# A chunked RWKV-7 scan: block-diagonal exponentials, operand products over 128 partitions, and inverse blocks placed by DMA

## The chip, the cores and the metric

The kernel runs on one core of a Trainium2 chip. A core has five engines with instruction streams of their own: TensorE (PE in the profile, with its weight loads as PEld), VectorE (DVE), ScalarE (ACT), GpSimd (POOL) and SyncE (SP), which in this kernel mostly starts DMAs. The metric is the device time of one execution in microseconds (us), the median over runs. All five engines wait for each other through semaphores.

## The reference, cut to what matters

One layer of a diffusion backbone: layer norms with modulation, one input projection that feeds three token mixers (Mamba-2 SSD, RWKV-7, GLA), an output projection, then a mixture of 64 experts. The change lies in the RWKV-7 mixer, a linear recurrence with a state of 64x64 per head, four heads, run forward and backward over 2304 tokens:

```python
def step(S, inp):
    r_t, w_t, k_t, v_t, kk_t, a_t = inp
    sa = -jnp.einsum('nhvk,nhk->nhv', S, kk_t)
    S = S * w_t[:, :, None, :] + sa[..., None] * (kk_t * a_t)[:, :, None, :] + v_t[..., None] * k_t[:, :, None, :]
    return S, jnp.einsum('nhvk,nhk->nhv', S, r_t)
y = unboth(_rwkv7_scan(both(r, r), both(w_f, w_b), both(k_f, k_b), both(v, v), both(kk, kk), both(a_f, a_b)))
```

Everything is computed in float32.

## The kernel before, in words

The kernel doesn't step through tokens. It cuts the 2304 tokens into 18 segments of 128 tokens, each of four chunks of 32. A segment of the forward direction (d=0) and one of the backward direction (d=1) are handled together as a pair, so there are 18 pairs in `run` (L609).

For each pair there is a preparation and a chain. The **chain** (`chain`, L624, and `chunk`, L646) carries the state through the four chunks of both directions: small matmuls, each waiting for a copy on ACT or an update on DVE of the one before, in 24 hops per pair. The **preparation** (`prep`, L494) makes, for the next pair, what the chain needs and the state doesn't enter:

- `first` (L522): cumulative sums of the log decays (L533, DVE; L534, POOL), their exponentials `rkE` (L536) and `rkEi` (L540) on ACT, and the operands `rkar` and `rkbk`, products of the loaded inputs `rkX` with these exponentials. The operands are stored block-diagonally by head: for heads in partitions 0-63 one set of columns, for those in 64-127 another, with zeros elsewhere that are written once. So a product covers 64 partitions. Per direction there are 8 of them on DVE (L548, L549) and 8 on POOL (L551, L550).
- `grams` (L554): PE products of the operands (L563), masked on DVE (L567, L569, L570), summed on POOL (L572) and stored to DRAM (L573). `btrans` (L575) transposes `rkbk` on PE.
- An inverse of 16x16 triangular blocks, for both directions at once: load of the blocks (L504), start value copied from a constant identity (L508), 30 small DVE operations in strict sequence (L513, L514), a transposed copy (L515), two stores to the DRAM buffer `rkTd` (L517).
- `diag` (L585), per direction: a load of the inverse blocks (`rkDT`, L588, 128x8x16), and a POOL multiplication by a 0/1 mask `hk` that spreads them block-diagonally over 128x1024 elements (`rkD`, L591).
- `inv1` (L595) and `inv2` (L602): two groups of matmuls per direction with `rkD` (L598, L605) that assemble the inverse of the 32x32 blocks, an ACT copy between them (`rkW`, L600) and a DVE subtraction behind them (`rkTb`, L607).

`PLAN` (L623) says at which hop of the chain the preparation takes a step. PE's order in this stage is fixed by hand: hops, preparation steps, and between them matmuls of the input projection for the other two mixers (L184, L203; `FILL`, 4, 3 or 4 matmuls per hop), which keep PE busy during the waits of the chain. So an instruction on PE that waits holds up all of these behind it. The orders of DVE, ACT, POOL and SP are made by a scheduler at build time from the program and its priorities. SP starts nearly all DMAs of the stage: inputs `rkX` (L489), values `rkuv` (L529), outputs `rkY` (L645), and the stores of the projection (`fo`, L189). The chain begins at its first hop with the operands of the pair; the D matmuls (L598) stand at hops 22 and 23 of the pair before.

Of the kernel before, what the change touches and what calls it, by code (L numbers as in the profile page):

```python
# [25 lines left out]
def ap(t, off, dims):  # L26
    return bass.AP(tensor=t.tensor, offset=t.offset + off, ap=[list(d) for d in dims])
# [377 lines left out]
def rk_masks(nc, pool, tmp):  # L405

    M={}
# [9 lines left out]
    hk=pool.tile([128,4,2],F32,name='hk')
    for q in range(4):
        for k in range(2):
            nc.vector.tensor_scalar(hk[:,q,k:k+1],h,float(q),None,op0=OP.is_equal)  # L420
            t=tmp.tile([128,1],F32,name=f'rkhk{q}{k}'); nc.vector.tensor_scalar(t,bs,float(k),None,op0=OP.is_equal)
            nc.vector.tensor_tensor(hk[:,q,k:k+1],hk[:,q,k:k+1],t,op=OP.mult)
    M['hk']=hk

    blk=tmp.tile([128,32],F32,name='blk16'); nc.vector.tensor_scalar(blk,bt[:,:32],bs,None,op0=OP.is_equal)
    for d in range(1):
        st=tmp.tile([128,128],F32,name=f'rkst{d}'); nc.vector.tensor_scalar(st,I,s,None,op0=(OP.is_gt if d==0 else OP.is_lt))
        ge=tmp.tile([128,128],F32,name=f'rkge{d}'); nc.vector.tensor_scalar(ge,I,s,None,op0=(OP.is_ge if d==0 else OP.is_le))

        lo=pool.tile([128,32],F32,name=f'mlo{d}'); nc.vector.tensor_tensor(lo,st[:,:32],blk,op=OP.mult)  # L430
        M['lo',d]=lo

        of=tmp.tile([128,32],F32,name=f'rkof{d}'); nc.vector.tensor_tensor(of,st[:,:32],lo,op=OP.subtract)
        m=pool.tile([128,2,32],F32,name=f'moff{d}')
        mi=tmp.tile([128,2,32],F32,name=f'mincl{d}')
        ms=tmp.tile([128,2,32],F32,name=f'mstr{d}')
        for half in range(2):
            P=slice(64*half,64*half+64)
            b=bd[P,64*half:64*half+64].rearrange("p (h t)->p h t",h=2)
            nc.vector.tensor_tensor(m[P],b,of[P,None,:].to_broadcast([64,2,32]),op=OP.mult)  # L440
            nc.vector.tensor_tensor(mi[P],b,ge[P,:64].rearrange("p (h t)->p h t",h=2),op=OP.mult)
            nc.vector.tensor_tensor(ms[P],b,st[P,:64].rearrange("p (h t)->p h t",h=2),op=OP.mult)
        M['off',d]=m

        gk=pool.tile([128,2,2,2,32],F32,name=f'mgk{d}')
        nc.vector.memset(gk,0.0)
        for p in range(2):
            B=slice(64*p,64*p+64); K=slice(64-64*p,128-64*p)
            nc.vector.tensor_copy(gk[K,p,p],ms[K])
            nc.vector.tensor_copy(gk[K,p,1-p],mi[K])  # L450
            nc.vector.tensor_copy(gk[B,p,1-p],mi[B])
        M['gk',d]=gk
        rm=pool.tile([128,8,32],F32,name=f'rm{d}')
        nc.vector.memset(rm,1.0)
        e=0 if d==0 else 31
        nc.vector.memset(rm[:,:,e:e+1],0.0)
        M['rm',d]=rm
# [3 lines left out]
class Rwkv:  # L461


    def __init__(s, tc, nc, const, sb, ps, dram, M, ident, OPS, V, Y, T):
        s.tc=tc; s.nc=nc; s.sb=sb; s.ps=ps; s.M=M; s.id=ident; s.OPS=OPS; s.V=V; s.Y=Y; s.T=T; s.dram=dram
        s.S=[None,None]
        s.st={}

        s.bufs={}; s.cnt={}
        for n,w,k in (('ar',1024,4),('bk',1024,2),('lf',512,2),('uv',512,4)):  # L470
            s.bufs[n]=[]; s.cnt[n]=0
            for i in range(k):
                t=const.tile([128,w],F32,name=f'rk{n}{i}')
                nc.gpsimd.memset(t,0.0)
                s.bufs[n].append(t)
        for d in range(2):
            s.S[d]=[const.tile([128,3,64],F32,name=f'rkS{d}{i}') for i in range(2)]
            for t in s.S[d]: nc.vector.memset(t,0.0)
        s.eye=const.tile([64,256],F32,name='rkI'); nc.gpsimd.memset(s.eye,0.0); nc.gpsimd.memset(s.eye[:,0:256:17],1.0)
    def buf(s,n):  # L480
        l=s.bufs[n]; t=l[s.cnt[n]%len(l)]; s.cnt[n]+=1
        return t
# [11 lines left out]
    def prep(s,segs):  # L494

        nc=s.nc; sb=s.sb
# [8 lines left out]
        Tn=sb.tile([64,2,16,16],F32,name='rkTn',bufs=1)  # L505
        tmp=sb.tile([64,64],F32,name='rktm',bufs=1)
        X0=Tn[:,0]
        nc.vector.tensor_copy(X0.rearrange("p a b->p (a b)"),s.eye)  # L508
        for j in range(15,0,-1):

            nr=j; ncl=16-j
# [10 lines left out]
    def first(s,d,seg):  # L522
# [7 lines left out]
        A=sb.tile([128,2,2,4,32],F32,name='rkA',bufs=1)  # L530
        cs=A[:,0].rearrange("p a u t->p a (u t)"); csx=A[:,1].rearrange("p a u t->p a (u t)")
        for p in range(2):
            nc.vector.tensor_tensor_scan(cs[:,p],M['rm',0].rearrange("p a t->p (a t)")[:,0:128],Xr[:,4,p],0.0,op0=OP.mult,op1=OP.add)  # L533
        nc.gpsimd.tensor_tensor(csx,cs,Xr[:,4],op=OP.subtract)  # L534
        E=sb.tile([128,2,2,4,32],F32,name='rkE',bufs=1)
        nc.scalar.activation(E.rearrange("p e a u t->p (e a u t)"),A.rearrange("p e a u t->p (e a u t)"),AF.Exp)  # L536
        G=sb.tile([128,2,4],F32,name=f'rkG{d}')
        nc.vector.tensor_copy(G,E[:,0,:,:,31])
        Ei=sb.tile([128,2,4,32],F32,name='rkEi',bufs=1)
        nc.scalar.activation(Ei.rearrange("p a u t->p (a u t)"),cs.rearrange("p a t->p (a t)"),AF.Exp,scale=-1.0)  # L540

# [12 lines left out]
    def grams(s,d,Ld,R):  # L554
# [29 lines left out]
        R.append(BKt)  # L584
    def diag(s,d,Td):  # L585
        nc=s.nc; sb=s.sb; M=s.M
        DT=sb.tile([128,2,4,16],F32,name='rkDT')
        nc.sync.dma_start(DT.rearrange("p a u j->p (a u) j"),ap(Td,d*16384,[[16,128],[2048,8],[1,16]]))  # L588
        D=sb.tile([128,8,4,2,16],F32,name='rkD',bufs=2)
        DTv=DT.rearrange("p a u j->p (a u) j")  # L590
        nc.gpsimd.tensor_tensor(D.rearrange("p au h k j->p au (h k) j"),DTv[:,:,None,:].to_broadcast([128,8,8,16]),  # L591
            M['hk'].rearrange("p h k->p (h k)")[:,None,:,None].to_broadcast([128,8,8,16]),op=OP.mult)
        Dv=D.rearrange("p (a u) h k j->p a u (h k j)",a=2)
        return Dv
    def inv1(s,d,R,Dv):  # L595
        nc=s.nc; lfm=R[4].rearrange("p (u c)->p u c",u=4)
# [82 lines left out]
class Ssd:  # L679
# [117 lines left out]
    def evac(s, pool, i, o, P, g):  # L797
# [1076 lines left out]
```

## Time and profile before

| what | value |
|---|---|
| three runs | 3887.36, 3897.21, 3893.46 us; median 3893.46 us |
| the profiled execution's own time | 3880.03 us |
| its span on the core | 3878.3 us |
| mean granted PE clock over the span | 0.947 of full |
| PE / DVE / ACT / POOL busy, share of the span | 90% / 68% / 43% / 33% |
| the scan stage | from about 647 to 1402 us of the span |
| its 17 preparations that run beside a chain | the first ends at about 695 us, the last at about 1388 us |

The times of the profile are microseconds from the start of the span. Busy time is summed over an engine's instructions; the idle time of an engine before an instruction is put down to what released it. PE's matmuls are pipelined, so a busy PE may be busy at less than its peak. The scan is one of several stages. The first 647 us project the input and prepare the RWKV inputs, the stage behind the scan (1402 to about 2055 us) does the SSD and GLA mixers and the output projection, and the rest is the mixture of experts. None of the others touches the changed lines, though the convolution of the projection shares the `fh` buffer (L806).

### The profile page before, as it was taken

The numbers are of one execution on the slowest core, as the hardware profiler recorded it, in microseconds if no ns is written. First come the engines' busy times: TensorE is split into PE (matmuls) and PEld (weight loads), VectorE is DVE, ScalarE is ACT, GpSimd is POOL, SyncE is SP. The second block draws the span as 40 slices with busy tenths as digits, with TensorE's granted clock in tenths as the row PEclk, the third lists the DMA queues.
The fourth block names the chain that finished last, engine by engine and source line by source line (L and its number), as shares of the span: only waits on it lengthen the run. The fifth ranks groups of instructions, "written<-read, shape, count | busy, mean of one in ns | idle before, by whom it ended". The sixth has DMA issues, their size and how long they took to land. (4 is left out here: it accounts for less than half of the span.)

```text
span 3878.3 us, 66200 instructions
## 1 busy us (share of the span) xinstructions
PE 3508.0 (90%) x23342; PEld 2956.9 (76%) x23342; DVE 2620.8 (68%) x6725; ACT 1658.7 (43%) x3899; POOL 1296.5 (33%) x1224
## 2 busy tenths in 40 slices
PE   8989887999799978996789899999999999999988
PEld 5978777888788856775577778887888878787863
DVE  4576865776777648676699966676556556666647
ACT  3565552554455534344466423343233323333315
POOL 0243543443334310110034643334433433333423
PEclk8999988999899988897799999999999999999999
DMA  7656544333433267766466557788878788788875
GB/s 233 215 188 211 171 152 138 85 98 110 112 86 90 65 183 220 250 193 211 143 210 196 182 143 227 216 253 235 249 233 242 236 254 253 217 279 238 255 231 187
DMA packets 498509, 745.77 MB, mean 192 GB/s; under 512 B 156704, under 2 KB 393312, under 8 KB 469216
## 3 DMA queue, kind: packets, MB, share of 16 engines
q1 hardware_dynamic: 438880, 522.20, 41.3%
q0 software_dynamic: 59296, 219.33, 21.8%
q8 instruction: 185, 3.03, 0.3%
q14 instruction: 148, 1.21, 0.1%
HBM read 524.31 MB, written 217.06 MB: 191 GB/s over the span
## 5 line engine op out<-in xcount | busy, mean ns | idle before, releaser
L1561 POOL DMA_INDIRECT d_f<-yo,en x162 | 317.7, 1961 | 569.7 <-DVE yo L1558 289.2
L1558 DVE SCALAR_TENSOR_TENSOR yo<-mm,f_w,g2r 128x512 f32<-128x512 f32 (+7 forms) x294 | 215.5, 745 | 250.1 <-PE mm L1556 146.8
L1577 POOL DMA_INDIRECT xg<-d_h,en x162 | 228.4, 1410 | 368.1 <-PE mm L1556 88.6
L184 PE MATMUL b<-uh,wh 128*128 128x384 f32 (+1 forms) x912 | 321.3, 358 | 11.5 <-ACT sce L805 5.0
L184 PE MATMUL b<-ul,wh 128*128 128x384 f32 (+1 forms) x912 | 322.5, 354 | 4.1 <-DMA ul<-d_ul 3.6
L184 PE MATMUL b<-uh,wl 128*128 128x384 f32 (+1 forms) x912 | 323.0, 354 | 0.0
L1448 DVE TENSOR_TENSOR w13l<-raw,w13h 128x2048 fp32r<-128x2048 f32 x100 | 228.6, 2286 | 27.5 <-ACT w13h L1448 27.3
L1328 POOL DMA_INDIRECT d_tab<-q_tk,q_slot x128 | 150.8, 1178 | 229.4 <-DVE q_slot L1321 133.7
L1556 PE MATMUL mm<-w2h,hWh 128*128 128x512 f32 (+3 forms) x480 | 208.2, 466 | 9.7 <-DVE hWh L1507 6.6
L1448 ACT ACTIVATE w13h<-raw 128x2048 fp32r<-128x2048 f32 x100 | 191.4, 1916 | 36.9 <-DMA raw<-in_exp_w_dram 34.6
L184 PEld LDWEIGHTS b<-uh,wh 128*128 128x128 f32 x912 | 178.1, 197 | 17.9 <-ACT sce L805 6.3
L1485 ACT ACTIVATE xWh<-g 128x512 fp32r<-128x512 f32 (+2 forms) x180 | 90.1, 538 | 220.6 <-PE g L1479 213.9
L184 PEld LDWEIGHTS b<-ul,wh 128*128 128x128 f32 x912 | 179.0, 196 | 6.7 <-DMA ul<-d_ul 3.8
L184 PEld LDWEIGHTS b<-uh,wl 128*128 128x128 f32 x912 | 179.0, 196 | 1.4
L1479 PE MATMUL g<-ident,xg 128*128 128x128 f32 (+9 forms) x1296 | 168.7, 263 | 9.1 <-DMA xg<-d_h,en 5.7
L1479 PEld LDWEIGHTS g<-ident,xg 128*128 128x128 f32 (+9 forms) x1296 | 143.0, 140 | 39.1 <-issue 17.3
L1516 PE MATMUL a<-w13l,xTh 128*128 128x512 f32 x400 | 162.7, 407 | 4.3 <-DVE w13l L1448 4.3
L1516 PE MATMUL a<-w13h,xTh 128*128 128x512 f32 x400 | 162.7, 407 | 0.3 <-DVE ov_kr L1356 0.3
L1516 PE MATMUL a<-w13h,xTl 128*128 128x512 f32 x400 | 159.6, 399 | 0.0
L1501 PE MATMUL c<-xWh,w13h 128*128 128x304 f32 (+7 forms) x448 | 150.1, 335 | 4.9 <-ACT w13h L1448 4.2
L1501 PE MATMUL c<-xWh,w13l 128*128 128x304 f32 (+7 forms) x448 | 146.8, 328 | 5.3 <-DVE w13l L1448 5.3
L1501 PE MATMUL a<-xWl,w13h 128*128 128x304 f32 (+7 forms) x448 | 151.2, 338 | 0.0
(712 smaller groups left out, 10487.9 us busy)
## 6 DMA issues: line engine op xcount, KB each, us to landing
raw<-in_exp_w_dram SPq DMA_DIRECT2D x147, 1024.0 KB
w13h<-in_exp_w_dram SPq DMA_DIRECT2D x30, 1024.0 KB
wr<-in_w_in_dram SPq DMA_DIRECT2D x46, 512.0 KB
uht<-d_uh POOLq DMA_DIRECT2D x32, 512.0 KB, 6.2
ult<-d_ul POOLq DMA_DIRECT2D x32, 512.0 KB, 6.2
mrw<-in_ada_w_dram SPq DMA_DIRECT2D x32, 512.0 KB
w2h<-in_exp_w_dram SPq DMA_DIRECT2D x15, 1024.0 KB
rkX<-d_ops SPq DMA_DIRECT2D x36, 384.0 KB
```

Of the source, the lines that this page charges most:

```text
L184: s.nc.tensor.matmul(P.rearrange("p (i t)->p i t",t=128),l,r[:,a//128:,k],start=(i==0),stop=(i==23)); i+=1
L1328: d=s.nc.gpsimd.indirect_dma_start(out=s.S['tab'],out_offset=bass.IndirectOffsetOnAxis(ap=s.slot[:,l,k:k+1],axis=0),in_=s.tk[:,l:l+1],in_o ...
L1448: pin(nc.scalar.activation(H,r,AF.Copy)); pin(nc.vector.tensor_tensor(L,r,rnd(H),op=OP.subtract))
L1479: for k in range(4): nc.tensor.transpose(p[:,k,:m],B['x'][:m,(4*g+k)*128:(4*g+k+1)*128],s.id[:m,:m])
L1485: nc.scalar.activation(H[:,a],p[:,:,:m],AF.Copy)
L1501: nc.tensor.matmul(p,w[a][:,j,k,c::2],x[b][:,k],start=(k+i==0),stop=(k==7 and i==len(ab)-1))
L1516: for a,b in ab: nc.tensor.matmul(p,a[:,k],b[:,:,k],start=(i==0),stop=(i==8*len(ab)-1)); i+=1
L1556: nc.tensor.matmul(r[:m],a[:,k],b[:,k,cs],start=(i==0),stop=(i==ni-1)); i+=1
L1558: else: nc.vector.scalar_tensor_tensor(o[:m,cs],r[:m],B['w'] if isinstance(B['w'],float) else B['w'][:m],s.g2[:m,cs],op0=OP.mult,op1=OP.mult)
L1561: d=nc.gpsimd.indirect_dma_start(out=s.S['f'],out_offset=bass.IndirectOffsetOnAxis(ap=B['en'][:m],axis=0),in_=o[:m],in_offset=None,compute ...
L1577: s.nc.gpsimd.indirect_dma_start(out=x[:m],out_offset=None,in_=s.S['h'],in_offset=bass.IndirectOffsetOnAxis(ap=B['en'][:m],axis=0))
```

## The change

1. The exponentials go to buffers that are block diagonal by head: `E` (128x1536, one buffer for both directions, zeroed once). Each direction takes four ACT instructions on 64 partitions (two for `rkE`, two for `rkEi`) in place of two on 128.
2. The operand products then cover all 128 partitions, with `rkX` broadcast over the head columns: 8 per direction, 128x256, all on DVE. The zeros are written anew by each product. POOL has none of them any more. `rkG` is the sum of the two head blocks instead of a copy.
3. The inverse blocks go from DRAM straight into their places in `rkD` (two buffers, zeroed once): 8 DMAs of 16x8x16 per direction on SP in place of one load and the POOL multiplication.
4. The start value of the inverse is set by two POOL memsets in place of the DVE copy. The mask `hk`, its 24 small DVE operations and the constant `rkI` go; the scan mask `rm` has half its columns (the other half wasn't used).
5. The buffer `fh` of the projection's convolution has one copy in place of two.

```diff
-        for n,w,k in (('ar',1024,4),('bk',1024,2),('lf',512,2),('uv',512,4)):
+        for n,w,k in (('ar',1024,4),('bk',1024,2),('lf',512,2),('uv',512,4),('D',1024,2),('E',1536,1)):
...
-        nc.vector.tensor_copy(X0.rearrange("p a b->p (a b)"),s.eye)
+        e=X0.rearrange("p a b->p (a b)"); nc.gpsimd.memset(e,0.0); nc.gpsimd.memset(e[:,0:256:17],1.0)
...
-        E=sb.tile([128,2,2,4,32],F32,name='rkE',bufs=1)
-        nc.scalar.activation(E.rearrange("p e a u t->p (e a u t)"),A.rearrange("p e a u t->p (e a u t)"),AF.Exp)
+        eb=s.buf('E').rearrange("p (e a u h t)->p e a u h t",e=3,a=2,u=4,h=2); E=eb[:,0:2]; Ei=eb[:,2]
+        for h in range(2):
+            P=slice(64*h,64*h+64)
+            nc.scalar.activation(E[P,:,:,:,h].rearrange("p e a u t->p (e a u) t"),A[P].rearrange("p e a u t->p (e a u) t"),AF.Exp)
+        for h in range(2):
+            P=slice(64*h,64*h+64)
+            nc.scalar.activation(Ei[P,:,:,h].rearrange("p a u t->p (a u) t"),cs[P].rearrange("p a (u t)->p (a u) t",u=4),AF.Exp,scale=-1.0)
         G=sb.tile([128,2,4],F32,name=f'rkG{d}')
-        nc.vector.tensor_copy(G,E[:,0,:,:,31])
-        Ei=sb.tile([128,2,4,32],F32,name='rkEi',bufs=1)
-        nc.scalar.activation(Ei.rearrange("p a u t->p (a u t)"),cs.rearrange("p a t->p (a t)"),AF.Exp,scale=-1.0)
+        nc.vector.tensor_tensor(G,E[:,0,:,:,0,31],E[:,0,:,:,1,31],op=OP.add)
...
-        for p in range(2):
-            for h in range(2):
-                P=slice(64*h,64*h+64)
-                nc.vector.tensor_tensor(ARb[P,p,:,p,h,:],x(P,1,p),E[P,1,p],op=OP.mult)
-                nc.vector.tensor_tensor(BKb[P,p,:,p,h,:],x(P,2,p),Ei[P,p],op=OP.mult)
-                nc.gpsimd.tensor_tensor(BKb[P,p,:,1-p,h,:],x(P,3,p),Ei[P,p],op=OP.mult)
-                nc.gpsimd.tensor_tensor(ARb[P,p,:,1-p,h,:],x(P,0,p),E[P,0,p],op=OP.mult)
+        x=lambda j,p: Xr[:,j,p,:].rearrange("p (u t)->p u t",t=32)[:,:,None,:].to_broadcast([128,4,2,32])
+        for o,j,a,e in ((ARb,1,0,E[:,1]),(BKb,2,0,Ei),(BKb,3,1,Ei),(ARb,0,1,E[:,0])):
+            for p in range(2): nc.vector.tensor_tensor(o[:,p,:,a^p],x(j,p),e[:,p],op=OP.mult)
...
-        DT=sb.tile([128,2,4,16],F32,name='rkDT')
-        nc.sync.dma_start(DT.rearrange("p a u j->p (a u) j"),ap(Td,d*16384,[[16,128],[2048,8],[1,16]]))
-        D=sb.tile([128,8,4,2,16],F32,name='rkD',bufs=2)
-        DTv=DT.rearrange("p a u j->p (a u) j")
-        nc.gpsimd.tensor_tensor(D.rearrange("p au h k j->p au (h k) j"),DTv[:,:,None,:].to_broadcast([128,8,8,16]),
-            M['hk'].rearrange("p h k->p (h k)")[:,None,:,None].to_broadcast([128,8,8,16]),op=OP.mult)
-        Dv=D.rearrange("p (a u) h k j->p a u (h k j)",a=2)
+        D=s.buf('D').rearrange("p (a b j)->p a b j",a=8,b=8)
+        for b in range(8): nc.sync.dma_start(D[16*b:16*b+16,:,b],ap(Td,d*16384+256*b,[[16,16],[2048,8],[1,16]]))
+        Dv=D.rearrange("p (a u) b j->p a u (b j)",a=2)
...
-        h=pool.tile([128,384],F32,name='fh',bufs=2)[:,:n]
+        h=pool.tile([128,384],F32,name='fh',bufs=1)[:,:n]
```

PE's order in the scan stays as it was. Two other orders matter for what follows. The first is SP's at the end of a preparation: stores of the inverse (`rkTd`), then the loads of its blocks, a store of the projection (`fo`), the next inputs (`rkX`), the outputs of the chain (`rkY`) and the values for a later pair (`rkuv`). Before:

```order
381 L189 DMA d_xbc<-fo 128x384
382 L517 DMA rkTd<-rkTn 32x2x256 x2
383 L588 DMA rkDT<-rkTd 128x8x16 x2
384 L189 DMA d_xbc<-fo 128x384
385 L489 DMA rkX<-d_ops 128x4x128
386 L529 DMA rkuv_5459<-d_v 32x4x64
387 L645 DMA d_yf<-rkY 32x4x64 x4
```

And with the change, where lines are numbered anew (L509 is the store of the inverse, L580 the load of its blocks, L633 the outputs, L521 the values):

```order
386 L509 DMA rkTd<-rkTn 32x2x256 x2
387 L580 DMA rkD_5434<-rkTd 16x8x16 x7
388 L189 DMA d_xbc<-fo 128x384
389 L580 DMA rkD_5434<-rkTd 16x8x16
390 L580 DMA rkD_5436<-rkTd 16x8x16 x8
391 L633 DMA d_yf<-rkY 32x4x64 x4
392 L521 DMA rkuv_5426<-d_v 32x4x64 x4
```

Two loads have become sixteen, a store of the projection stands between them, and the load of `rkX` has moved behind the outputs and values. A store of the projection stands among the sixteen in 12 of the 17 pairs, in 7 of these inside the first direction's eight.

The second is ACT's between the two directions' D matmuls: the copies `rkW`, which the matmuls of L605 read, the outputs `rkY`, the scaled state `rkSG` and the exponentials `rkE` of the next preparation. Before:

```order
933 L600 ACTIVATE rkW<-b_8863 128x512
934 L640 ACTIVATE rkY<-b_8428 64x256
935 L641 ACTIVATE rkY<-b_8428 64x256
936 L656 ACTIVATE rkSG_8942<-rkS_5467,rkG_8453 128x64 x2
937 L536 ACTIVATE rkE<-rkA 128x512
938 L600 ACTIVATE rkW<-b_8879 128x512
```

And with the change:

```order
931 L588 ACTIVATE rkW<-b_8791 128x512
932 L628 ACTIVATE rkY<-b_8363 64x256
933 L629 ACTIVATE rkY<-b_8363 64x256
934 L644 ACTIVATE rkSG_8870<-rkS_5440,rkG_8390 128x64 x2
935 L531 ACTIVATE rkE_5438<-rkA 64x16x32 x2
936 L588 ACTIVATE rkW<-b_8807 128x512
```

The exponentials stand in the same place, ahead of the second direction's `rkW`, as two instructions in place of one.

Behind the scan, where the scheduler also orders PE, about 2000 rows of PE's order and 1600 of DVE's stand elsewhere than before, though nothing in that stage's own code has changed.

## Rows read from the trace of the kernel before

**Rows 1.** Busy time of each engine in two stretches, scan and the stage behind
```profile
core 0: us, PE busy (x) PEld busy (x) DVE busy (x) ACT busy (x) POOL busy (x), PEclk, DMA share, GB/s
647.00:1402.00 755.00, 680.91 (x5320) 609.03 (x5318) 547.09 (x1641) 379.13 (x1229) 285.68 (x392) 0.96 0.34 89
1402.00:2055.00 653.00, 531.28 (x5822) 429.34 (x5820) 486.64 (x1477) 301.40 (x935) 85.15 (x120) 0.87 0.67 212
```
**Rows 2.** PE's waits in the scan: sum us, count, longest us
```profile
PE b L598 <- POOL rkD L591: 43.6, 13, 18.6
PE b L661 <- ACT rkR L659: 10.9, 10, 3.1
PE b L581 <- DVE rkGK L570: 10.2, 11, 1.8
PE b L666 <- ACT rkuv L663: 3.1, 5, 1.5
```
**Rows 3.** Timeline of PE, one pair's D matmuls: start, us, [idle before]
```profile
729.01 1.16 PE L598 MATMUL b<-rkD,rklf 128*128 128x128 f32 x8 [1.70 <-POOL rkD L591]
730.97 1.08 PE L598 MATMUL b<-rkD,rklf 128*128 128x128 f32 x8
```
**Rows 4.** Timeline of SP's DMA issues
```profile
679.70 1.01 SPq L588 DMA_DIRECT2D rkDT<-rkTd  x2
704.84 0.36 SPq L573 DMA_DIRECT2D rkLd<-rkLc  x1
706.65 0.45 SPq L504 DMA_DIRECT2D rkSy<-rkLd  x1
724.16 1.02 SPq L588 DMA_DIRECT2D rkDT<-rkTd  x2
726.00 0.36 SPq L489 DMA_DIRECT2D rkX<-d_ops  x1
734.53 1.82 SPq L529 DMA_DIRECT2D rkuv<-d_vr  x4
1375.66 1.01 SPq L588 DMA_DIRECT2D rkDT<-rkTd  x2
```
**Rows 5.** Timeline of POOL, the spreading multiplications of the first, second, last pair
```profile
684.27 4.11 POOL L591 TENSOR_TENSOR rkD<-rkDT,hk 128x1024 f32<-128x1024 f32 x2
727.03 3.81 POOL L591 TENSOR_TENSOR rkD<-rkDT,hk 128x1024 f32<-128x1024 f32 x2 [1.05 <-DMA rkDT<-rkTd]
1378.09 1.92 POOL L591 TENSOR_TENSOR rkD<-rkDT,hk 128x1024 f32<-128x1024 f32 x1 [5.86 <-DMA rkDT<-rkTd]
```
**Rows 6.** Groups in the scan: busy us, mean ns | idle before, releasers
```profile
L548 DVE TENSOR_TENSOR rkar<-rkX,rkE 64x128 f32<-64x128 f32 x128 | 68.0, 531 | 30.0 <-ACT rkE L536 18.5 <-PE b L654 10.2
L549 DVE TENSOR_TENSOR rkbk<-rkX,rkEi 64x128 f32<-64x128 f32 x128 | 53.8, 420 | 2.8 <-ACT rkEi L540 1.1 <-PE b L581 0.2
L569 DVE TENSOR_TENSOR rklf<-b,moff 64x256 f32<-64x256 f32 x68 | 28.7, 422 | 1.5
L551 POOL TENSOR_TENSOR rkar<-rkX,rkE 64x128 f32<-64x128 f32 x128 | 62.3, 486 | 123.2 <-PE b L654 83.6 <-ACT rkE L536 33.4
```
**Rows 7.** One line's instructions over the program: min/median/max ns
```profile
L549 DVE TENSOR_TENSOR rkbk<-rkX,rkEi x144: 272/434/2430, 559.7 to 1321.6; 64x128 f32<-64x128 f32 x144
L536 ACT ACTIVATE rkE<-rkA x36: 612/629/632, 563.1 to 1340.6; 128x512 f32<-128x512 f32 x36
L540 ACT ACTIVATE rkEi<-rkA x36: 400/417/420, 559.2 to 1319.8; 128x256 f32<-128x256 f32 x36
L513 DVE TENSOR_TENSOR rktm<-rkSy,rkTn x270: 102/204/2352, 597.0 to 1366.7; 64x15 f32<-64x15 f32 x18, 64x39 f32<-64x39 f32 x18, 64x55 f32<-64x55 f32 x18, 64x63 f32<-64x63 f32 x18
```
**Rows 8.** SP's waits in the scan: sum us, count, longest us
```profile
SPq L189 <- DVE rkS L668: 33.0, 9, 6.9
```
**Rows 9.** Semaphore waits of PE's load queue at one matmul line: ns
```profile
L652 PEldq EVENT_SEMAPHORE  x71: 51/51/51, 644.4 to 1386.5; - x71
```

More of the change, by code (lines that the diff above doesn't have):

```diff
@@ L416, in rk_masks @@
     bs=tmp.tile([128,1],F32,name='rkbs'); nc.vector.tensor_scalar(bs,s,16.0,None,op0=OP.is_ge)
[L417 to L423, printed above, removed]
     blk=tmp.tile([128,32],F32,name='blk16'); nc.vector.tensor_scalar(blk,bt[:,:32],bs,None,op0=OP.is_equal)
@@ L452, in rk_masks @@
         M['gk',d]=gk
-        rm=pool.tile([128,8,32],F32,name=f'rm{d}')
+        rm=pool.tile([128,4,32],F32,name=f'rm{d}')
         nc.vector.memset(rm,1.0)
@@ L478, in __init__ @@
             for t in s.S[d]: nc.vector.memset(t,0.0)
-        s.eye=const.tile([64,256],F32,name='rkI'); nc.gpsimd.memset(s.eye,0.0); nc.gpsimd.memset(s.eye[:,0:256:17],1.0)
     def buf(s,n):
@@ L532, in first @@
         for p in range(2):
-            nc.vector.tensor_tensor_scan(cs[:,p],M['rm',0].rearrange("p a t->p (a t)")[:,0:128],Xr[:,4,p],0.0,op0=OP.mult,op1=OP.add)
+            nc.vector.tensor_tensor_scan(cs[:,p],M['rm',0].rearrange("p a t->p (a t)"),Xr[:,4,p],0.0,op0=OP.mult,op1=OP.add)
         nc.gpsimd.tensor_tensor(csx,cs,Xr[:,4],op=OP.subtract)
-        E=sb.tile([128,2,2,4,32],F32,name='rkE',bufs=1)
-        nc.scalar.activation(E.rearrange("p e a u t->p (e a u t)"),A.rearrange("p e a u t->p (e a u t)"),AF.Exp)
+        eb=s.buf('E').rearrange("p (e a u h t)->p e a u h t",e=3,a=2,u=4,h=2); E=eb[:,0:2]; Ei=eb[:,2]
@@ L540, in first @@
-        nc.scalar.activation(Ei.rearrange("p a u t->p (a u t)"),cs.rearrange("p a t->p (a t)"),AF.Exp,scale=-1.0)
+        nc.vector.tensor_tensor(G,E[:,0,:,:,0,31],E[:,0,:,:,1,31],op=OP.add)
         ARb=arb.rearrange("p (q u a h t)->p q u a h t",q=2,u=4,a=2,h=2)
         BKb=bkb.rearrange("p (q u a h t)->p q u a h t",q=2,u=4,a=2,h=2)
-        x=lambda P,j,p: Xr[P,j,p,:].rearrange("p (u t)->p u t",t=32)
-        for p in range(2):
-            for h in range(2):
-                P=slice(64*h,64*h+64)
-                nc.vector.tensor_tensor(ARb[P,p,:,p,h,:],x(P,1,p),E[P,1,p],op=OP.mult)
-                nc.vector.tensor_tensor(BKb[P,p,:,p,h,:],x(P,2,p),Ei[P,p],op=OP.mult)
-                nc.gpsimd.tensor_tensor(BKb[P,p,:,1-p,h,:],x(P,3,p),Ei[P,p],op=OP.mult)
-                nc.gpsimd.tensor_tensor(ARb[P,p,:,1-p,h,:],x(P,0,p),E[P,0,p],op=OP.mult)
+        x=lambda j,p: Xr[:,j,p,:].rearrange("p (u t)->p u t",t=32)[:,:,None,:].to_broadcast([128,4,2,32])
```

## The prediction

> **What bounds the kernel now.** I read the busy times by stretch first. In the scan, which alone holds the changed lines, PE is busy for 680.9 of 755 us, DVE for 547.1, ACT for 379.1, POOL for 285.7, at a granted clock of 0.96, with DMA at a third [rows 1]. So PE bounds the stage, and since its order is fixed by hand with filling work, at most the 74 us in which it is idle can be won. What I look for is therefore not how much work the other engines lose or gain, but which of their results PE waits for.
>
> PE's waits come second. Of the 74 us, 43.6 are the wait of the D matmuls (L598) for the spread inverse `rkD`, in 13 pieces, of which one is 18.6 us. The chain's waits for ACT are 10.9 and 3.1 us, those for the gram masks 10.2 [rows 2]. So the path to look at is: inverse on DVE, store, load, spreading, D matmul. Third, the timelines along this path. In the pair at 724 us SP issues the two loads at 724.16 in 1.02 us [rows 4], POOL multiplies from 727.03, 3.81 us for both directions [rows 5], and PE begins at 729.01 after a wait of 1.70 [rows 3]. The second direction's group of matmuls begins 1.96 us later without any wait [rows 3]: its `rkD` is done 1.9 us after the first one, as PE wants it.
>
> **Term A: placing the inverse blocks.** Let f be the start of the first load's issue. Before, the first `rkD` is ready at f+6.6 in the first pair of the stage (679.70; 684.27 and half of 4.11), f+4.8 in the pair at 724, f+4.3 in the last (1375.66; 1378.09 + 1.92) [rows 4, 5]; over all 17 pairs, worked out alike from such rows, the mean is f+5.2, and the second stands at f+7.1. With the change, eight issues must go out before the first `rkD` is complete. Four issues to SBUF in one row take 1.82 us, 0.455 each, and the way from a small DMA's issue to an issue that waited for its landing is 706.65 - 704.84 = 1.81 us [rows 4]. So the first is ready at f + 7 x 0.455 + 1.81 + 0.15 (a mean for the store among them: one issue in 7 of 17 pairs) = f+5.15, the second at f + 15 x 0.455 + 1.81 + 0.26 = f+8.9. The first hardly moves, the second comes 1.8 us later. I put both into the 17 pairs one by one, PE being ready at the start of its first L598 less the wait in front of it, and the second group wanted 2 to 4 us behind the first. The first groups then wait 38.2 us in all, the second ones 16.1: together 54.3 in place of 43.6, which is **+10.7 us**. With the shortest issue in the rows, 0.36, the same table gives -7; with 0.51 (half of the pair of `rkDT` issues) +23. I keep 0.455, the row of a load with short runs into SBUF.
>
> At this place the Trainium skill, "DMA: Bandwidth & Descriptors", section "Anatomy of one DMA — SWDGE (gpsimd) path", speaks against the change: a DMA costs about 2 us however little it moves, so many small ones are poor. Here the 1.81 us agree; with 2.0 in their place the sum would rise by an estimated 0.2 us in the pairs in which PE waits.
>
> **Term B: an earlier inverse.** POOL loses 16 products per direction pair (for half of them the row has 62.3 us over 16 pairs) [rows 6] and two multiplications of 1.92 us [rows 5]. DVE's work per pair hardly changes: 16 products of 64x128 at 420 to 531 ns, 7.6 us, become 16 of 128x256, whose nearest row is 64x256 with 422 ns [rows 6], 6.8 us; the copy of the start value goes. But DVE operations beside POOL ones are stretched: the 64x128 product takes 272 ns at the least, 434 in the middle and 2430 at the most, and an operation of the inverse between 102 and 2352 [rows 7]. POOL's `rkbk` products run beside the first steps of the inverse; its long weight splits of the projection do too, and these stay. I put the gain at 0.5 us per pair, as two or three of the thirty operations have such a neighbour and lose some 0.2 us each. With f half a microsecond earlier the table falls from 54.3 to 47.3, **-7 us**. Bounds: nothing, and 1.5 us per pair (34.6, -20).
>
> The Trainium skill's "SBUF — State Buffer", section "SBUF: two separate sides", gives a rule for this: DVE and GpSimd share a port pair under an exclusive lock, held for a whole instruction, and the loser is blocked entirely. The 272 against 2430 ns agree. By it every removed POOL product that met a DVE operation gives its whole duration back, which is the first rival below.
>
> **Term C: exponentials.** Per direction two instructions of 512 and two of 256 columns take the place of one each. With the durations unchanged by the number of partitions (my assumption, 629 and 417 ns [rows 7]) ACT works 1.05 us longer per direction. One added instruction stands ahead of the second direction's `rkW`, which the second half of the inverse (L605) reads, and the chain's copies stand behind all of them. But the chain's waits for ACT are small, 14 us in all [rows 2], since PE has filling work in front of each. I take **+3 us**; below zero it can't go, as nothing leaves ACT, and if every added microsecond reached PE it would be +35 (17 x 2 x 1.05).
>
> **Term D: more to wait for.** The D matmuls, and the DVE subtraction behind them, now wait for up to eight DMA semaphores instead of one of POOL. A wait of PE's load queue that is already satisfied is 51 ns [rows 9]; seven more of them on two engines and for two directions are 1.4 us per pair, 24 us if nothing hid them. The load queue runs ahead of PE, and where PE waits for data anyway they pass meanwhile, so **+2 us**, bounds 0 and 24.
>
> **At nothing** I put the memsets on POOL (it has the freed time, and the old inverse is stored long before), the missing constants, and the single `fh` buffer: its next writer comes a projection tile later, several microseconds in this stage. If that cover is gone, ACT waits for one DVE operation per tile, which is a part of term C's upper bound. The `rkX` load now stands behind the D loads, the outputs and the values, some 22 issues, 10 us by 0.455. Its readers, the scans, come after the DVE subtraction and then have a whole pair, about 43 us, so I take 0; what it costs without this cover is part of the second rival. The stage behind, where PE idles 122 of 653 us [rows 1], is reordered by the scheduler without a change in its work: 0, with 20 us either way, a sixth of that idle time.
>
> **Sum:** 10.7 - 7 + 3 + 2 = about +9 us on 3880.03, the profiled execution's own time, so 3889; the median of the runs is 13.4 above that execution, so the forecast is **3902 us** at the runs' level. About 0.3%, 11.7 us, is what a measurement of this kernel can tell from no change; 3902 lies within it, on the slow side.
>
> **Rivals.** *1, POOL's relief decides (faster).* The inverse ends 1.5 us earlier in every pair, ACT and the semaphores are hidden: -20 from the table and about -2 from the gram masks, where PE waits 10.2 us for DVE [rows 2]: 3871. For it speaks the spread in [rows 7]; against it, that POOL's 2.4-us weight splits, which stay, account for the longest of these, and that the 18.6-us stall, nearly half of the wait, is one event.
>
> *2, SP's queue decides (slower).* SP issues in order, and a store of the projection that isn't ready holds up the D loads behind it. It stands among them in 12 pairs. Such stores wait 33.0 us in 9 places now, up to 6.9 [rows 8], 3.7 in the mean. If 2 us of this fall on the D loads in 12 pairs, that is +24, and with 6 more where `rkX` comes late: +30, 3923. It decides from the point at which such a store is held for over 1 us in most of these 12 pairs, since then the 11.7 us are passed. Against it: most stores are ready when SP comes to them.
>
> *3, the reordered stage behind the scan decides.* 20 us either way, 3873 or 3913 at an unchanged scan. Nothing in the profile says which.
>
> *That the change doesn't do what it says* I exclude: its matmuls and DMAs stand in the built order.
>
> **Chances.** Forecast 0.44 (its own range 3888 to 3916: within 0.29, slower by over 0.3% 0.15); rival 1 0.27 (faster 0.24, within 0.03); rival 2 0.20 (slower 0.18, within 0.02); rival 3 0.09 (a third each). Together: faster 0.27, within 0.37, slower 0.36. The range goes from 3868, just past rival 1, to 3934, where terms A and C with their upper thirds (+23, +12) and rival 2 meet.
>
> **What would show it.** Right: the D matmuls wait in the scan for the DMAs of `rkD` by 45 to 55 us, with new waits of 1 to 2 us at the second group; POOL's busy time in the scan falls by about 190 us (125 of products, 65 of multiplications); a product of 128x256 takes 0.40 to 0.45 us; ACT rises by 36 us; PE's work stays at 681 us. Wrong: if the wait for `rkD` falls below 35 us, rival 1; if SP's stores wait among the D loads by over 2 us, rival 2; if the scan's length is unchanged but the total isn't, rival 3. The weakest point is the landing of sixteen small DMAs: if these take clearly longer than 1.81 us under load, every pair pays for it.

## The result: 1.7% slower

| | median us | runs |
|---|---|---|
| before | 3893.46 | 3887.36 to 3897.21 |
| changed | 3957.53 | 3952.90 to 3974.68 |

The ratio is 1.0171, 95% interval 1.0153 to 1.0190; timed a second time on another occasion it was 1.0158 (1.0124 to 1.0193). The forecast was 3902, the range ended at 3934. The first profile of the changed kernel fell on an execution of 5518 us, not in the table, in which the chip granted PE 0.56 of its clock in the mean, so the profile shown here is of the second occasion, an execution with a span of 3954.6 us.

**Where the time went.** I cut both spans at the same two pieces of work: the scan from the first to the last state update of the chain (L666 before, L654 now), and the stage behind it from there to the first transposition of the experts' inputs (further than the second stretch of [rows 1], which ends at 2055). Columns as in [rows 1]. Before:

```profile
656.10:1405.60 749.50, 675.17 (x5274) 603.23 (x5272) 539.38 (x1621) 378.99 (x1228) 284.07 (x389) 0.96 0.34 89
1405.60:2266.70 861.10, 718.83 (x6764) 584.77 (x6763) 677.00 (x2349) 397.22 (x1238) 199.47 (x216) 0.89 0.63 203
```

And changed:

```profile
660.00:1447.40 787.40, 678.80 (x5272) 607.40 (x5271) 491.91 (x1605) 415.82 (x1290) 104.78 (x131) 0.95 0.33 85
1447.40:2334.60 887.20, 733.90 (x6763) 595.06 (x6763) 682.01 (x2354) 399.95 (x1238) 194.49 (x216) 0.87 0.62 198
```

The scan is 37.9 us longer, nearly all of it idle time of PE (74.3 to 108.6 us); PE's busy time rose by 3.6. The stage behind, whose work is the same, is 26.1 us longer. The experts, compared with an execution near the median (the kernel with one `fh` buffer, below), take the same within 2 us. In the scan DVE has lost 47 us of busy time, POOL 179, ACT has gained 37: off the bounding engine, and worth nothing by themselves. PE's waits in the changed scan, against [rows 2] (sum us, count, longest us; lines numbered as in the changed kernel, L586 the D matmuls, L649 the chain's):

```profile
PE b L586 <- DMA rkD<-rkTd: 73.8, 22, 23.4
...
PE b L649 <- ACT rkR L647: 7.3, 10, 1.6
PE b L586 <- DMA rkuv<-d_v: 4.1, 1, 4.1
PE b L586 <- issue: 4.0, 2, 3.2
...
PE b L586 <- DMA d_yf<-rkY: 1.8, 1, 1.8
```

Taken together (the last three stand before D matmuls too, where another DMA landed last or the profile names none) the D matmuls' wait has gone from 43.6 us in 13 places to 84 in 26. The chain's wait for ACT has not grown. One pair shows it, the one that answers to [rows 3, 4]. SP's issues (start, us, count):

```profile
728.49 5.04 SPq L580 DMA_DIRECT2D rkD<-rkTd  x11
734.37 2.33 SPq L580 DMA_DIRECT2D rkD<-rkTd  x5
```

And PE's two groups of D matmuls (start, us, idle before):

```profile
733.93 2.05 PE L586 MATMUL b<-rkD,rklf 128*128 128x128 f32 x8 [3.14 <-DMA rkD<-rkTd]
738.37 1.13 PE L586 MATMUL b<-rkD,rklf 128*128 128x128 f32 x8 [0.88 <-DMA rkD<-rkTd]
```

The last of the sixteen issues ends at 736.70, and the second group can start only 1.67 us behind that. Before, it started without a wait 1.96 us behind the first [rows 3]. And the first group, after a wait of 3.14 us, takes 2.05 us where 1.13 is usual: the granted clock was 0.50 there, the lower of the two levels (1.2 and 2.4 GHz), and 1.00 again in the second group. Columns as in [rows 1], the clock third from the end:

```profile
733.93:735.98 2.05, 2.05 (x9) 2.05 (x10) 0.02 (x1) 0.00 (x0) 0.00 (x0) 0.50 0.37 109
738.37:739.50 1.13, 1.13 (x9) 1.13 (x10) 0.00 (x0) 1.12 (x3) 0.00 (x0) 1.00 0.28 64
```

From the start of a pair's first D matmul to the last gram matmul of the next preparation, summed over the 16 such stretches, before 236.8 us pass, of which PE idles 4.9; changed it is 270.1, idle 26.7. That is 21.8 us more idle and 11.6 more busy time (in the rest of the scan PE was busy 8 us less, which I have not traced). In the rest, from the gram matmuls to the D matmuls, the mean of a pair is 28.7 us before and 28.9 after. So nearly all of the scan's loss lies behind the first blocks' arrival: the second direction's blocks and the low clock after the waits.

### The profile page after: what moved, and what is told of

It reads as the page before. It is cut to its first block, busy times and chain, and to the rows that moved or that the text cites. A ratio compares the mean times of both kernels' runs of the same rounds, so it can differ in the third digit from the quotient of the medians.

```text
span 5516.6 us, 66258 instructions
## 1 busy us (share of the span) xinstructions
PE 5328.4 (97%) x23342; PEld 3851.9 (70%) x23342; DVE 2614.9 (47%) x6683; ACT 1731.2 (31%) x3971; POOL 1059.0 (19%) x937
## 4 chain that ended last, share of the span: by engine, by line
PE 56%; issue 5%; DMA 2%; DVE 1%; ACT 1%; POOL 0%; SPq 0%; POOLq 0%; DVEq 0%; ACTq 0%
PE mm L1544 13%; PE a L1504 10%; PE c L1489 8%; PE a L1489 8%; PE mm L1236 5%; PE g L1467 4%; PE b L230 1%; PE c L1275 1%; PE mm L1536 1%; DMA d_f<-yo,en 1%; PE b L871 0%; DMA uht<-d_uh 0%; PE a L1246 0%; PE c L1522 0%; PE b L859 0%
## 5 line engine op out<-in xcount | busy, mean ns | idle before, releaser
L184 PE MATMUL b<-uh,wl 128*128 128x384 f32 (+1 forms) x912 | 446.1, 489 | 0.0
L184 PE MATMUL b<-ul,wh 128*128 128x384 f32 (+1 forms) x912 | 443.9, 487 | 0.3 <-DVE ul L139 0.3
L184 PE MATMUL b<-uh,wh 128*128 128x384 f32 (+1 forms) x912 | 441.8, 490 | 1.3 <-ACT wh L163 0.9
L1544 PE MATMUL mm<-w2h,hWh 128*128 128x512 f32 (+3 forms) x480 | 307.9, 679 | 0.0
L1467 PE MATMUL g<-ident,xg 128*128 128x128 f32 (+9 forms) x1296 | 255.8, 351 | 2.7 <-issue 1.3
L1504 PE MATMUL a<-w13h,xTh 128*128 128x512 f32 x400 | 230.3, 576 | 0.0
L1504 PE MATMUL a<-w13l,xTh 128*128 128x512 f32 x400 | 229.1, 573 | 0.0
L1504 PE MATMUL a<-w13h,xTl 128*128 128x512 f32 x400 | 224.0, 560 | 0.0
L656 DVE SCALAR_TENSOR_TENSOR rkS<-b,rkG,rkSG 128x64 f32<-128x64 f32 x288 | 68.6, 279 | 310.4 <-PE b L654 289.0
L1489 PE MATMUL c<-xWl,w13h 128*128 128x304 f32 (+7 forms) x448 | 204.6, 457 | 0.0
```

Of the source, the lines that this page charges most:

```text
L184: s.nc.tensor.matmul(P.rearrange("p (i t)->p i t",t=128),l,r[:,a//128:,k],start=(i==0),stop=(i==23)); i+=1
L1467: for k in range(4): nc.tensor.transpose(p[:,k,:m],B['x'][:m,(4*g+k)*128:(4*g+k+1)*128],s.id[:m,:m])
L1489: nc.tensor.matmul(p,w[a][:,j,k,c::2],x[b][:,k],start=(k+i==0),stop=(k==7 and i==len(ab)-1))
L1504: for a,b in ab: nc.tensor.matmul(p,a[:,k],b[:,:,k],start=(i==0),stop=(i==8*len(ab)-1)); i+=1
L1544: nc.tensor.matmul(r[:m],a[:,k],b[:,k,cs],start=(i==0),stop=(i==ni-1)); i+=1
```

## The experiments

All were timed against the kernel before on the same chip. "Scan" and "behind" are cut as above, "order" is PE's order behind the scan against the kernel before; in the scan it was never moved except by the name of what it reads. "Scan" and "behind" are from one profiled execution each, the ratios from 4 to 12 runs.

| kernel | ratio (95%) | scan | behind | order |
|---|---|---|---|---|
| before | | 749.5 | 861.1 | |
| one `fh` buffer | 0.9999 (0.9983-1.0014) | 749.5 | 866.3 | same |
| start value by DVE memsets | 0.9994 (0.9982-1.0006) | 746.0 | 859.3 | same |
| start value by POOL memsets | 1.0025 (1.0011-1.0039) | 749.5 | 886.6 | moved |
| changed, without the DMAs | 1.0055 (1.0035-1.0075) | 749.1 | 881.9 | moved |
| changed | 1.0158 (1.0124-1.0193) | 787.4 | 887.2 | moved |
| before with the DMAs | 1.0191 (1.0166-1.0216) | 797.1 | 898.8 | moved |
| changed, 32 DMAs | 1.0580 (1.0555-1.0606) | 938.9 | 891.9 | moved |
| changed, 8 joint DMAs | 1.0195 (1.0158-1.0233) | 787.0 | 907.8 | moved |
| before, 8 joint DMAs | 1.0143 (1.0115-1.0172) | 767.2 | 908.8 | moved |
| 8 joint DMAs, SP and ACT | 1.0124 (1.0096-1.0152) | 771.7 | 909.5 | moved |
| 16 DMAs, d=1 on POOL | 1.0190 (1.0174-1.0207) | 792.8 | 894.6 | moved |
| 16 DMAs, SP and POOL by turns | 1.0159 (1.0144-1.0174) | 774.8 | 893.2 | moved |

**Which part.** The changed kernel again, its parts alone, and the one buffer alone.

> The changed kernel as it is, for a profile at full clock, since the one there was taken at 0.56. Expected 3958 us, ratio 1.017. Theory S (scan): the scan is some 50 to 70 us longer than its 755 us, with PE's work there near 681 us and the wait of the D matmuls (L586) for the DMAs of rkD at 60 us or more. Theory C (clock): PE's waits grow by little, but the granted clock is lower in some stretch (0.939 in the mean against 0.947), so that PE's own busy time is 30 us or more longer. Theory R (reorder): the scan is as long as before within 10 us, and the stage behind it is 40 us or more longer.

```diff
  before, with this (and the buffer for D in place of the mask hk):
-        nc.sync.dma_start(DT.rearrange("p a u j->p (a u) j"),ap(Td,d*16384,[[16,128],[2048,8],[1,16]]))
...
+        for b in range(8): nc.sync.dma_start(D[16*b:16*b+16,:,b],ap(Td,d*16384+256*b,[[16,16],[2048,8],[1,16]]))
```

> The kernel before with the 16 DMAs per pair that place the inverse blocks, in place of load and multiplication, and nothing else. If the DMAs are the cause (theory S): about 3940 to 3960 us, ratio 1.012 to 1.017. If the operand products and exponentials are: within 0.3% of before. My term A alone would give about +11 us, ratio 1.003.

> The changed kernel with load and POOL multiplication for the inverse blocks put back; exponentials, products, memsets and the single fh buffer stay changed. If the DMAs are the cause: ratio 0.995 to 1.003. If exponentials and products (ACT and DVE busier at the chain's copies) are: 1.010 or more. If the reordered stage behind the scan is, both this and the kernel with the DMAs alone may be slow, by different amounts.

 (Edit: the reverse of the diff above, on the changed kernel.)

```diff
-        h=pool.tile([128,384],F32,name='fh',bufs=2)[:,:n]
+        h=pool.tile([128,384],F32,name='fh',bufs=1)[:,:n]
```

> The kernel before with one fh buffer in place of two; the order of all engines is unchanged. I cost this at nothing: ratio within 1.000 +- 0.003. If the single buffer makes ACT wait for DVE at each projection tile and with it the chain's copies: up to 1.008.

The scan with the DMAs alone, then with the other edits alone, columns as in [rows 1]:

```profile
662.90:1460.00 797.10, 697.20 (x5273) 622.61 (x5272) 525.24 (x1621) 380.96 (x1228) 218.41 (x355) 0.93 0.32 84
662.10:1411.20 749.10, 670.26 (x5272) 597.86 (x5272) 512.31 (x1605) 418.58 (x1290) 171.86 (x165) 0.97 0.35 89
```

The DMAs alone make the scan 47.6 us longer, the other edits leave it as it was (-0.4). So the scan's loss is the DMAs', all of it (theory S). The parts don't add up to the whole: beside the DMAs the other edits take back 9.7 us (797.1 to 787.4). The clock (theory C) is a follower: with the DMAs alone the granted clock in the scan is 0.93, and PE is busy 22 us longer for the same instructions. Theory R holds beside S, not in its place: without the DMAs the kernel is still 0.55% slower, with the loss behind the scan. One `fh` buffer costs nothing.

**Issue or transfer.** Theory I says that the time comes from issuing sixteen DMAs one behind the other, theory P that the small pieces need it however they are issued. Dose first:

```diff
-        for b in range(8): nc.sync.dma_start(D[16*b:16*b+16,:,b],ap(Td,d*16384+256*b,[[16,16],[2048,8],[1,16]]))
+        for b in range(8):
+            for g in range(2): nc.sync.dma_start(D[16*b:16*b+16,4*g:4*g+4,b],ap(Td,d*16384+256*b+8192*g,[[16,16],[2048,4],[1,16]]))
```

> The changed kernel with twice the DMAs, 16 per direction of 16x4x16, the same bytes in the same 64-byte pieces, all on SP. Theory I: the first blocks are ready at f + 15 x 0.47 + 1.8 = f+8.9, the second at f+16.4; each first group waits some 3.5 us longer and each second one some 3.7, so the scan is 100 to 130 us longer than with 16, and the total 4050 to 4090. Theory P: the scan within 15 us of 790, the total about 3960.

The same bytes in twice the DMAs: the scan grows by 151.5 us, the D matmuls' wait for `rkD` from 73.8 to 179.5. SP in one pair, then PE there (start, us, count; idle before):

```profile
744.18 5.94 SPq L581 DMA_DIRECT2D rkD<-rkTd  x13
750.63 8.87 SPq L581 DMA_DIRECT2D rkD<-rkTd  x19
```

```profile
753.46 2.04 PE L587 MATMUL b<-rkD,rklf 128*128 128x128 f32 x8 [6.45 <-DMA rkD<-rkTd]
760.95 2.05 PE L587 MATMUL b<-rkD,rklf 128*128 128x128 f32 x8 [3.64 <-DMA rkD<-rkTd]
```

An issue takes 8.87/19 = 0.467 us, and the blocks come at f+9.3 and f+16.8 in this pair (f the first issue's start), where I foresaw 8.9 and 16.4 and P no change. The total is above I's 4050 to 4090 since the granted clock fell to 0.86 and PE was busy 54 us longer (732.9 us in place of 678.8), which neither theory had:

```profile
669.00:1607.90 938.90, 732.91 (x5273) 656.81 (x5272) 494.91 (x1603) 417.73 (x1289) 104.95 (x131) 0.86 0.27 71
```

Then half the DMAs:

```diff
-        for b in range(8): nc.sync.dma_start(D[16*b:16*b+16,:,b],ap(Td,d*16384+256*b,[[16,16],[2048,8],[1,16]]))
+        for b in range(8): nc.sync.dma_start(D[16*b:16*b+16,:,b],ap(Td,256*b,[[16,16],[2048,16],[1,16]]))
```

> The kernel before (its products on DVE and POOL) with 8 DMAs per pair that place the blocks of both directions. Theory I: the scan is 30 us or more shorter than with 16 DMAs on the same kernel (799.9 us there), near 765; total about 3935. Theory P: scan at 790 to 800, total about 3965.

> The changed kernel with 8 DMAs per pair in place of 16: each places the blocks of both directions at once (16x16x16 into one buffer for both directions; it has one copy, as the two of before together). The same bytes in the same 64-byte pieces. Theory I (the issue of 16 DMAs one behind the other on SP, 0.47 us each, makes the second direction's blocks late): the waits of the second groups of D matmuls, about 22 us, go, and with them some 12 us that PE spends at the low clock behind them; the scan is near 757 us in place of 790, the total 3915 to 3930, with up to 15 us either way from the stage behind. Theory P (the small pieces take their time in the DMA engines however they are issued): waits and scan stay, total 3945 to 3960.

On the kernel before, the scan is 767.2 in place of 797.1, as theory I had it. On the changed kernel it is 787.0, not the 757 that I gave. The second groups' waits are gone there too (idle behind the first D matmul 4.3 us in place of 26.7). But the first groups wait 72.3 us. The same pair, SP and then PE:

```profile
724.83 3.82 SPq L580 DMA_DIRECT2D rkD<-rkTd  x8
```

```profile
730.68 1.39 PE L585 MATMUL b<-rkD,rklf 128*128 128x128 f32 x8 [4.39 <-DMA rkD<-rkTd]
733.67 1.60 PE L585 MATMUL b<-rkD,rklf 128*128 128x128 f32 x8
```

A joint DMA waits for both stores of the inverse (the first issue mostly 2.2 us behind the store's start, not 1.7), and lands some 2.0 us behind the last issue, here 730.68 - 728.65. The first blocks come 30.0 us behind the gram matmuls, 1.1 later than with sixteen. So fewer issues moved the wait from the second group to the first.

**Other queues.**

```diff
+        for b in range(8): (nc.sync,nc.scalar)[b%2].dma_start(...)   # joint, 8 in all
+        for b in range(8): (nc.sync,nc.gpsimd)[d].dma_start(...)     # d=1 on POOL
+        for b in range(8): (nc.sync,nc.gpsimd)[b%2].dma_start(...)   # by turns
```

> The 8 joint DMAs issued by turns from SP and ACT, four each. Theory I: the first blocks are ready 4 x 0.47 = 1.9 us earlier than with eight on SP, which takes 15 to 25 us off the waits of the first groups of D matmuls, unless ACT, where the chain's copies stand, pays for the four issues: between 10 us more than with all eight on SP and 25 us less. Theory P: the same as with all eight on SP.

> The changed kernel with the second direction's eight DMAs issued by POOL, which has little to do in the scan now; the first direction's stay on SP. Theory I (issue on one queue): the second groups' waits, 22 us, and the low clock behind them go, the first groups stay as they are: scan 755 to 765 in place of 790, total 3915 to 3940. Theory P (the small pieces need the DMA engines' time): what the second set gains, the first loses, since both now move at once: scan 780 or more.

> The changed kernel with the eight DMAs of each direction issued by turns from SP and POOL. Theory I: the first blocks are ready at f + 3 x 0.47 + 1.8 = f+3.2 in place of f+5.2 to 6.3, the second at f+5.1: the scan is 735 to 750, below the kernel before. Theory P: the first blocks come at f+5 or later all the same; scan 755 or more. Eight joint DMAs from two queues have not come earlier than from one, which speaks for P here.

None gave back what I had expected of it. With joint DMAs on SP and ACT, SP's four are out 1.8 us behind f in most pairs, but the first blocks still come at f+4.8 to f+6.5 in nine of the fifteen pairs that waited, and between f+3.8 and f+9.6 in the others. This looks like P and isn't, since in thirteen of them the blocks are there 1.7 to 2.7 us behind the last of the eight issues: ACT, in order, puts its issues between the chain's copies. In the pair at 1276.93 (start, us), then PE:

```profile
1276.93 0.36 ACTq L580 DMA_DIRECT2D rkD<-rkTd  x1
1277.45 0.35 ACTq L580 DMA_DIRECT2D rkD<-rkTd  x1
1278.37 0.31 ACTq L580 DMA_DIRECT2D rkD<-rkTd  x1
1280.24 0.31 ACTq L580 DMA_DIRECT2D rkD<-rkTd  x1
```

```profile
1282.25 1.02 PE L585 MATMUL b<-rkD,rklf 128*128 128x128 f32 x7 [0.82 <-DMA rkD<-rkTd]
```

The last issue ends at f+3.6, and the blocks are there 1.7 us later. With d=1 on POOL the second groups' waits fall from 21.4 us to 7.5, but others take their place (sum us, count, longest us; in the changed kernel the waits for `rkTb` and `rkGK` at L554 were 2.4 and 3.2 us):

```profile
PE b L586 <- DMA rkD<-rkTd: 56.3, 14, 24.8
PE b L593 <- ACT rkW L588: 11.4, 6, 2.8
PE b L554 <- DVE rkTb L595: 7.0, 5, 2.6
PE b L554 <- DVE rkGK L561: 6.4, 5, 2.0
```

By turns on SP and POOL the first blocks are there at f+4.3 to f+4.9 in seven of the pairs that waited, against f+5.2 to f+6.3, and the wait for `rkD` falls to 38.4 us. That is earlier, as theory I foretold and P did not, but I had given f+3.2 and a scan of 735 to 750, and the 774.8 measured lie in P's range. POOL explains most of the gap to f+3.2: in the pair at 729.72 its four issues start 0.48 us behind SP's and take 0.53 each, which by the same sum gives an estimated f+4.4. And 13.1 us of waits before D matmuls, mostly second groups, remain of which the profile names no releaser, and 13.7 for `rkTb`. The trace shows where the second groups' waits come from: these groups start 2.0 to 5.9 us behind POOL's last issue, while SP's sets in the changed kernel were there 1.4 to 2.2 us behind theirs. So what POOL issues lands later (by the profile 2.4 us from issue to landing in the middle, 4.2 at most), and POOL has other work in front of it. In the pair at 683.73, POOL and then PE:

```profile
684.25 2.13 POOL L580 DMA_DIRECT2D rkD<-rkTd  x4 [15.59 <-DMA rkTd<-rkTn]
686.39 2.36 POOL L164 TENSOR_TENSOR wl<-wr,wh 128x1024 fp32r<-128x1024 f32 x1
688.68 2.09 POOL L580 DMA_DIRECT2D rkD<-rkTd  x4
694.85 1.38 PE L586 MATMUL b<-rkD,rklf 128*128 128x128 f32 x5 [4.74 <-issue]
```

For the waits further on ACT shows one reason, the exponentials that stand ahead of the second `rkW` (start, us, count):

```profile
738.16 1.25 ACT L531 ACTIVATE rkE<-rkA 64x512 f32<-64x512 f32 x2
739.44 0.60 ACT L588 ACTIVATE rkW<-b 128x512 f32<-128x512 f32 x1
```

The rest of these new waits I have not traced further.

**The stage behind.** The smallest edit that moves the scheduler's order there, and its twin that doesn't:

```diff
-        nc.vector.tensor_copy(X0.rearrange("p a b->p (a b)"),s.eye)
+        e=X0.rearrange("p a b->p (a b)"); nc.gpsimd.memset(e,0.0); nc.gpsimd.memset(e[:,0:256:17],1.0)
```

> The kernel before with only the start value of the inverse set by two POOL memsets in place of the DVE copy. The order of the scan hardly moves, but the scheduler moves 327 rows of PE's order in the stage behind. Theory O (any move of that order costs what the changed kernels lose behind the scan, 15 to 25 us): scan within 5 us of 752, the stage behind 10 to 25 us longer, ratio 1.003 to 1.006. Theory W (the loss behind the scan comes from work that the products or DMAs leave behind): ratio 0.998 to 1.002.

> The kernel before with the start value of the inverse set by two memsets on DVE, which leaves PE's and SP's order as it was. Theory O (the order behind the scan is what costs there): the stage behind as before within 7 us, ratio 0.998 to 1.002. Theory W (the memsets themselves cost): as with the memsets on POOL, ratio 1.0025.

On POOL (order moved), then on DVE (order as before), the stage behind, columns as in [rows 1]:

```profile
1408.60:2295.20 886.60, 730.56 (x6763) 592.31 (x6763) 678.34 (x2348) 399.00 (x1238) 195.74 (x216) 0.88 0.62 197
```

```profile
1411.50:2270.80 859.30, 713.04 (x6763) 579.52 (x6762) 676.85 (x2348) 397.38 (x1238) 198.30 (x216) 0.89 0.64 204
```

The same memsets, 27 us apart in these two executions, with no difference in the scan's work. Over all runs the two differ by less, 0.31% or some 12 us (1.0025 against 0.9994), so 27 is no price of a moved order. All ten kernels whose order moved have 882 to 910 us here, the three with the old order 859 to 866, and two of the ten (the DMAs on the kernel before) have no memset on POOL. So theory O holds: the loss behind the scan goes with the order, not with the new work. What in the order costs it stays open; PE idles more (156 against 146 us in this twin) and at a lower clock is busy longer. No version beat the kernel before beyond its interval.

## Why the prediction was wrong, step by step

- **Term A failed by its size**, and in the second direction above all. I had the first blocks at f+5.15 and the second at f+8.9; in the pairs in which PE waited they came at f+5.7 and f+10.3 in the mean. The price of an issue (0.455; 7.40 us for sixteen) and the landing behind the last one (1.81; 1.4 to 2.3 measured) were right. Wrong was how much stands between: the sixteen issues take 7.4 us where nothing interrupts them and 8.5 in the mean over 17 pairs, with stores and waits of SP among them, and in four pairs one issue that took 1.4 to 1.7 us by itself, for a reason that no run shows. The same table with 5.7 and 10.3 gives +32 us in place of +10.7, close to the scan's +38. That it comes so close is luck in part: it has 44.9 us for the first groups and 30.9 for the second, and measured were 62.6 and 21.3, since PE came to the first groups 0.9 us sooner.
- **What the term left out:** PE at the lower clock behind a wait. I had priced a wait at its own length. Behind the D matmuls PE was busy 11.6 us longer for the same work; over the whole scan only 3.6 of it is left here, but 22 with the DMAs alone.
- **Term B's mechanism was right in part and its gain didn't come.** Both forms of a product now, min/median/max ns:

```profile
L542 DVE TENSOR_TENSOR rkbk<-rkX,rkE x128: 397/415/427, 660.6 to 1357.9; 128x256 f32<-128x256 f32 x128
L542 DVE TENSOR_TENSOR rkar<-rkX,rkE x128: 405/418/2599, 680.7 to 1381.9; 128x256 f32<-128x256 f32 x128
```

  In the scan 11 products took over 0.9 us before, each beside an instruction of POOL, nine of them beside the spreading multiplication; now there are three, each beside one of POOL's weight splits (L164), which stay. So DVE was relieved where the spreading multiplication went, and hardly in the inverse. Its steps that take over 0.4 us all stand beside POOL's work in both kernels, 26 before and 15 now, but most of what they lose is lost to the splits: over 0.2 us each, in sum 24.8 us before and 23.5 now. The stretch moved from step to step, two of them before and now (busy us, mean ns | idle before):

```profile
L513 DVE TENSOR_TENSOR rktm<-rkSy,rkTn 64x39 f32<-64x39 f32 x34 | 14.3, 422 | 1.0
L513 DVE TENSOR_TENSOR rktm<-rkSy,rkTn 64x48 f32<-64x48 f32 x34 | 6.8, 199 | 1.0
L505 DVE TENSOR_TENSOR rktm<-rkSy,rkTn 64x39 f32<-64x39 f32 x34 | 6.9, 204 | 0.9
L505 DVE TENSOR_TENSOR rktm<-rkSy,rkTn 64x48 f32<-64x48 f32 x34 | 13.1, 385 | 1.0
```

  The inverse's own steps take 7.6 us a pair in place of 8.0, and DVE's other work among them 4.9 in place of 4.2. So the inverse ends 20.2 us behind the gram matmuls, 20.4 before, and the first load's issue starts no earlier (23.0, 22.9). What became faster is PE's own way to the D matmuls, 25.3 us in place of 26.2, and it waits there for that much longer. So rival 1 is out, and not only because of the DMAs: with load and multiplication put back the D matmuls wait for 49.5 us, against 43.6 before. The rule of the Trainium skill's "SBUF — State Buffer", section "SBUF: two separate sides", by which a POOL operation blocks a DVE one for its whole length, agrees: products beside the spreading multiplication of 1.92 us [rows 5] took 1.75 to 2.35 us, those beside a split of some 2.4 us 2.58 to 2.60.
- **Term C:** ACT's added work, 36.8 us, came as forecast (627 and 414 ns on 64 partitions, as on 128 [rows 7]), and no cost of it shows: the chain's wait for ACT is 7.3 us, not above the 10.9 of [rows 2], and without the DMAs, ACT being 39.6 us busier than before, the scan is as long as before (749.1).
- **Term D** can't be told apart in these runs.
- **At nothing:** `fh` was. The memsets weren't, though not by their work: on POOL they move the order behind the scan, and the ratio is 1.0025.
- **The stage behind, put at 0 with 20 us either way, failed:** it is 21 to 26 us longer, and it was longer in every kernel with a moved order. I had taken a moved order as a coin toss and had no evidence for the half in which it wins.
- **Rival 2** had the place and the side, SP's queue, with 30 us for the scan (38 measured). Its mechanism, stores held among the loads, is only a part of that: a store stands among the sixteen in 12 pairs, as the order said, but SP's gap there is over 1 us in four of them (0.5 where the store is ready, 2.44 at the longest), not in most, and the dose of issues alone moves the scan by 150. (The 33.0 us of [rows 8] are one of two such rows: stores of the same line waited 31.7 us more in 7 places behind L514.) A loss of rival 2's size and one of rival 3's came together. I had priced the two as alternatives, and that is why the range, wide enough for either, missed by 23 us. Its end at 3934 follows from no sum: terms A and C at their upper thirds with B and D give 3923, and so does rival 2.

The Trainium skill's "DMA: Bandwidth & Descriptors", section "Anatomy of one DMA — SWDGE (gpsimd) path", which is on DMAs issued from GpSimd, puts the fixed cost of a DMA almost wholly into the landing, with about 50 ns for the dispatch. Here POOL is held for 0.53 us per issue and SP, whose path that section doesn't describe, for 0.46, and it is this that adds up; the measurement decides.

## What to carry to other kernels

Count the DMAs that one result needs, and their place in the queue: sixteen small ones cost sixteen issues in a row plus whatever stands between, and the last one sets the time. A saving on an engine that doesn't bound becomes a longer wait if what the bounding engine waits for comes no earlier. Where a scheduler orders the rest of the program, time a neutral edit that moves its order, before a small difference is put down to the change, and take the size from many runs and not from one profile of each.

## What the runs showed of the hardware

- SP issued small DMAs every 0.45 to 0.48 us, eight to nineteen in a row, but for single issues of 1.4 to 1.7 us; POOL every 0.53. Behind the last issue of a set on SP the waiting group started 1.4 to 2.3 us later, 2.0 to 5.9 where POOL had issued half of the set.
- Eight D matmuls take 1.13 us at a granted clock of 1.00 and 2.05 at 0.50. In the changed scan they came at 0.50 behind waits of 3.14 and 3.78 us and at 1.00 behind one of 3.16. With 32 DMAs per pair, where nearly every first and second group waits for over 3 us, the mean granted clock of the scan fell from 0.95 to 0.86.
- A multiplication on DVE took 0.415 us for 128x256, and another line's for 64x256 0.422 in the mean; an exponential on ACT took the same on 64 partitions as on 128 (627 and 629 ns).
- Beside POOL's multiplication of 1.92 us a DVE product that takes 0.27 us at the least took 1.75 to 2.35.
